# GpSimd's split subtractions moved to VectorE, and three small steps rewritten, in a fused two-layer kernel

## The chip, the cores and the metric

One core of a Trainium2 chip runs the whole program in one launch. The metric is the device time of an execution in microseconds (us). The engines are TensorE (PE, with its weight loads PEld), VectorE (DVE), ScalarE (ACT), GpSimd (POOL) and SyncE (SP, which here only issues transfers).

## The reference, cut to what matters

Everything is float32, with 256 tokens of width 1024. Two layers, each a mixer and a layer of experts, are followed by a block of attention and feed-forward.

```python
for i in range(2):
    h = mlstm_mixer(x, ...) if i == 0 else gla_mixer(x, ...)
    x = layer_norm(ALPHA * x + h, ln_g[i, 0], ln_b[i, 0])
    y = ec_moe(x, ...)            # router, top-32 tokens for each of 16 experts, gate/up/down
    x = layer_norm(ALPHA * x + y, ln_g[i, 1], ln_b[i, 1])
return second_block(x, ...)       # rms norm, attention, rms norm, convolution, gated feed-forward

def mlstm_mixer(x, w_in, gate_b, norm_g, w_out):     # 4 heads, both directions
    z = x @ w_in                                     # q, k, v, o, gates
    logD = where(mask, b[t] - b[s] + i[s], -inf)     # causal mask (mirrored when going backwards)
    s = (q k^T) * exp(logD - m)                      # E = exp(logD - m) is what the kernel calls E
    h = head_norm(s v / max(|den|, exp(-m)))
    return (sigmoid(o) * h) @ w_out

def gla_mixer(x, w_in, gate_w, gate_b, norm_g, w_out):   # gated linear attention, both directions
    loga = log_sigmoid(...) / 16                     # per key channel, so decays are products over time
    ...
    return (silu(r) * head_norm(o)) @ w_out
```

## The kernel before

**Matmuls in three passes.** Each float32 operand of a large projection is split into a high part h (rounded to the matmul's format fp32r) and a low part l = src - h, and `mm3` (L331) issues h*h, h*l and l*h: L332, L333, L334. Activations are xh, xl; weights wh, wl. `split_w` (L287) makes h and l of half a weight unit, 128x1024 elements: ScalarE copies h (L297; in six cases VectorE, L295) and the engine at the end of the list `sub` subtracts (L298). `sub` is set to one of the lists of `ENG`: 0 is VectorE alone, 1 GpSimd alone, 2 both in turn.

**Weights** come as 1 MB units, in one stream, into a pool of 25 slots (`slab()` for activations and `take()` for units draw on the same slots). SP issues the next unit as soon as a slot is free, so a unit's release by its reader starts a transfer.

**Order of the work.** The program is written stage by stage and a scheduler sets the order of each engine's instructions; engines then run their own list in that order.

**The first mixer** (`mlstm`, L510): projections of q and k (transposed, `proj_T`), gates, E for both directions (L574 on VectorE, exp on ScalarE at L576, the triangular masks by GpSimd's affine_select at L580), scores L587 times E (L588 to L591), projection of v, heads (L613 to L621), head norm, then `mixer_out` (L483): projection of the output gate, product, output projection `token_out`. `columns` (L1107), called in between, turns small parameters into columns and multiplies the router's weights by the norm's gain and bias (L1114, GpSimd, tile `rw` in the slab `gpad`); L1124 sums these tables over the 1024 rows with 16 matmuls by a matrix of ones.

**The second mixer** (`gla`, L625) has seven levels in which chunk pairs of doubled length are joined: at each level ScalarE copies k (L706), TensorE multiplies (L715, later L719), and `upd` (L726) multiplies four strided halves of the slabs `kst` and `qs` in place by decay products (L731, four instructions of 128x512 elements per level); L741 makes the next products. The projections of v and of the output gate stand between the levels on TensorE.

**The expert layers** (`moe`) stream 192 units each. At their end `last_down` sums the last expert's output and calls `split_early`, which splits the first one and a half units of what follows, and `norm_split` (L1067) makes the layer norm: statistics, `rsqrt` (L435, nine VectorE instructions on 128x2 values, L442 to L452), a diagonal matrix (L1082), (x - mean) * gain (L1090), a transposing matmul (L1093), and the split into h (ScalarE, L312) and l (VectorE, L313). After it `finish0` and `finish1` make the normalised rows with GpSimd (L1173; L1227 and L1228).

Of the kernel before, what the change touches and what calls it, by code (L numbers as in the profile page):

```python
# [10 lines left out]
F32 = mybir.dt.float32  # L11
# [3 lines left out]
AF = mybir.ActivationFunctionType  # L15
OP = mybir.AluOpType
# [28 lines left out]
def two_layer_mixer_moe_then_attention_kernel(  # L45
# [254 lines left out]

    def transposed(src, use, bank=aux):
# [41 lines left out]

    def split_early():
        open_split()
        sub[:] = ENG[1]
        early.append(iter(list(split_unit())))
        ws = split_unit()
        early.insert(0, chain([next(ws)], ws))
        sub[:] = [nc.vector]  # L350

    def proj_T(xh, xl):
        lo_last = len(early) > 1
        if len(early) == 1 and not tr[1:]:
            tr.append(0)
            wl_last = 1
        else:
            wl_last = 0
        ws = early.pop() if early else split_unit()
        pb = acc()  # L360
        for f in range(2):
            wh, wl = next(ws)
            o = pb[:, f * S:(f + 1) * S]
            if f < lo_last:
                for k in range(8):
                    nc.tensor.matmul(o, wh[:, k, :], xh[:, k, :], start=k == 0, stop=False)
                    mm = nc.tensor.matmul(o, wl[:, k, :], xh[:, k, :], start=False, stop=False)
                for k in range(8):
                    with tc.issue_after(mm.ins):
                        mm = nc.tensor.matmul(o, wh[:, k, :], xl[:, k, :], start=False, stop=k == 7)  # L370
                last[:] = [mm]
                continue
            if wl_last:
# [12 lines left out]
        return pb  # L386
# [96 lines left out]
    def mixer_out(hv, g, func, xh, xl, res, mm, late, ac):  # L483
# [9 lines left out]
        sub[:] = ENG[1]  # L493
# [15 lines left out]
        sub[:] = ENG[2]  # L509
# [5 lines left out]
    def mlstm(xh, xl, res, after_qk):  # L515
# [37 lines left out]

        qk = slab()
# [13 lines left out]
        for d in range(2):  # L568
            e = slab()
# [7 lines left out]
            for h in range(4):  # L577
                for o0 in (0, 256):
                    sg = 1 if d == 0 else -1
                    nc.gpsimd.affine_select(ev[:, h, o0:o0 + P], ev[:, h, o0:o0 + P], pattern=[[sg, P]],  # L580
                                            compare_op=OP.is_ge, fill=0.0, base=0, channel_multiplier=-sg)
            E.append(ev)
# [42 lines left out]
        return mixer_out(hv, V_MLSTM_G, AF.Sigmoid, xh, xl, res, mm, [2, 4], ac)  # L625


    def gla(xh, xl, x1, prep):
# [38 lines left out]
        sub[:] = [(nc.vector, nc.gpsimd)[j] for j in [0, 1]]  # L667
# [26 lines left out]
        for lev in range(7):  # L694
# [31 lines left out]
            def upd(eng, base, d, half, g, ghalf):  # L726
                dst = bass.AP(tensor=base.tensor, offset=base.offset + d * 1024 + half * hh,
                              ap=[list(base.ap[0]), [2 * hh, nb], [1, hh]])
                src = bass.AP(tensor=gprod.tensor, offset=gprod.offset + g * gs + ghalf,
                              ap=[list(ga[0]), [2, nb], [0, hh]])  # L730
                eng.tensor_tensor(dst, dst, src, op=OP.mult)  # L731
# [37 lines left out]
        sub[:] = ENG[2]  # L769
# [19 lines left out]
        return mixer_out(hv, V_GLA_G, AF.Silu, xh, xl, x1, mm, [2, 3], mm)  # L789
# [276 lines left out]
    def norm_split(sums, bn, o, gb, bc, mm):  # L1066
# [13 lines left out]
        for t in range(2):  # L1080
            ts = slice(t * P, (t + 1) * P)
            dgi = nc.vector.tensor_scalar(dg[:, ts], ident, rs2[:, t:t + 1], None, op0=OP.mult)  # L1082
        for t in range(2):
            rs = rs2[:, t:t + 1]
            ts = slice(t * P, (t + 1) * P)
            for c in range(2):
                for u in (2 * c, 2 * c + 1):
                    us = slice(256 * u, 256 * u + 256)
                    with tc.issue_after(dgi.ins):
                        nc.vector.scalar_tensor_tensor(o[:, t, us], sums[u][:, t, :], mv[:, t, 0:1], gb[:, us],  # L1090
                                                       op0=OP.subtract, op1=OP.mult)
                for k in range(4 * c, 4 * c + 4):
                    nc.tensor.matmul(pvs[2 * t + c][:, k % 4, :], o[:, t, k * P:(k + 1) * P], dg[:, ts],  # L1093
                                     start=False, stop=k % 4 == 3)
                hi = split_part(h[:, 4 * c:4 * c + 4, ts], l[:, 4 * c:4 * c + 4, ts], pvs[2 * t + c])
            mvs.append(mv[:, t, :])
            rss.append(rs)
# [9 lines left out]
    def columns():  # L1107
# [4 lines left out]
        for i in range(2):  # L1112
            for j, v in ((1, V_LN_B), (0, V_LN_G)):
                nc.gpsimd.tensor_tensor(rw[:, i, :, j, :], rw[:, i, :, 0, :],  # L1114
                                        cols[:, v + 16 * i:v + 16 * i + 8, None].to_broadcast([P, 8, 16]), op=OP.mult)
            nc.gpsimd.tensor_copy(rt[:, 8 * i:8 * i + 8, :], rw[:, i, :, 0, :])
# [5 lines left out]
        for i in range(2):  # L1122
            for k in range(8):
# [4 lines left out]
        nc.vector.tensor_copy(rsum.rearrange("p i a e -> p (i a e)"), pb[:, :64])  # L1128
# [357 lines left out]
```

## Time and profile before

| | |
|---|---|
| median of 3 runs | 1531.09 us (1530.36 to 1531.26) |
| the profiled execution | 1529.58 us, of which the span of its instructions is 1527.8 us |
| mean granted TensorE clock | 0.869 of full speed |
| busy: PE, PEld | 1304.0 us (85%), 916.9 us (60%) |
| busy: DVE, ACT, POOL | 551.7 us (36%), 374.9 us (25%), 203.7 us (13%) |
| read from HBM | 489.61 MB, 321 GB/s over the span |

How to read the rows further down. A row of the timeline is: start us, duration us, engine, line, operation, what it writes <- what it reads, shape, xcount of instructions merged into it, and in brackets how long the engine was idle before it and who ended that. A row of the windows is: stretch, its length, then busy us and (xcount) of PE, PEld, DVE, ACT, POOL, then the granted TensorE clock, the busy share of the 16 DMA engines, and GB/s. Of the waits: who waited for whom, us in total, times, longest. Of the groups: line, engine, operation, names, shapes, xcount | busy us, mean ns of one | idle before. A float32 matmul that is not fp32r stands as two or more passes in the counts of PE.

### The profile page before, as it was taken

The page shows a single profiled execution, that of the slowest core. Times are in us where ns is not written, and L with a number is a line of the kernel's source. Part 1 is how long each engine was busy: PE and PEld are TensorE (multiplying, and loading weights), DVE is VectorE, ACT ScalarE, POOL GpSimd, SP SyncE. Part 2 cuts the span into 40 slices and gives each one's busy share as a digit, 9 for nine tenths or more (in the row PEclk, how much of TensorE's full clock was granted, in tenths as well). Part 3 has the DMA queues.
Part 4 walks back from the last instruction along what each step waited for, and adds up shares of the span by engine and source line. Part 5 has one row for each costly group of instructions (what it writes and reads, how often), then busy time and mean ns, then how long its engine had stood idle before and what let it go on. Part 6 is the DMA issues. An engine that isn't in the chain of part 4 may idle for free.

```text
span 1527.8 us, 27209 instructions
## 1 busy us (share of the span) xinstructions
PE 1304.0 (85%) x11779; PEld 916.9 (60%) x11779; DVE 551.7 (36%) x1103; ACT 374.9 (25%) x601; POOL 203.7 (13%) x142
## 2 busy tenths in 40 slices
PE   9899977667667677989996758999998899999998
PEld 8787644222222225878753426666564798799997
DVE  5467110011001005686520100200111685687776
ACT  5244100000000001655310000000000365365554
POOL 1243002100100001543100210000002400011000
PEclk9899998677677779999998776867679899999999
DMA  9749899999999999736899999999999943646500
GB/s 287 299 165 359 345 420 421 420 421 421 399 421 421 421 420 356 247 112 249 318 414 421 420 413 421 420 421 420 420 420 387 356 153 106 217 146 203 182 1 28
DMA packets 129303, 492.42 MB, mean 322 GB/s; under 512 B 11570, under 2 KB 68037, under 8 KB 81056
## 3 DMA queue, kind: packets, MB, share of 16 engines
q1 hardware_dynamic: 127216, 489.93, 81.7%
q8 instruction: 92, 1.51, 0.4%
q0 software_dynamic: 864, 0.66, 0.2%
q10 hardware_dynamic: 1104, 0.10, 0.1%
q14 instruction: 27, 0.22, 0.0%
HBM read 489.61 MB, written 1.05 MB: 321 GB/s over the span
## 4 chain that ended last, share of the span: by engine, by line
PE 53%; DMA 36%; DVE 8%; ACT 2%; issue 1%; POOL 0%; SPq 0%; DVEq 0%; ACTq 0%
DMA unit<-in_moe_w_up_dram 13%; DMA unit<-in_moe_w_down_dram 11%; DMA unit<-in_moe_w_gate_dram 11%; PE acc L964 8%; PE acc L333 7%; PE acc L332 7%; PE acc L334 7%; PE aux L1197 6%; PE aux L1011 4%; PE aux L333 1%; PE aux L332 1%; PE aux L334 1%; DVE slab L731 1%; PE aux L919 1%; PE aux L1029 1%
## 5 line engine op out<-in xcount | busy, mean ns | idle before, releaser
L964 PE MATMUL acc<-unit,slab 128*32 128x256 f32 x3840 | 317.5, 472 | 107.5 <-DMA unit<-in_moe_w_up_dram 56.1
L964 PEld LDWEIGHTS acc<-unit,slab 128*32 128x32 f32 x3840 | 129.9, 129 | 291.4 <-DMA unit<-in_moe_w_up_dram 89.8
L333 PE MATMUL acc<-slab 128*128 128x256 f32 (+1 forms) x912 | 282.7, 310 | 3.8 <-DVE slab L298 3.6
L332 PE MATMUL acc<-slab 128*128 128x256 f32 (+1 forms) x912 | 277.9, 310 | 2.1 <-DVE slab L295 1.4
L334 PE MATMUL acc<-slab 128*128 128x256 f32 (+1 forms) x912 | 278.9, 309 | 0.5 <-DVE slab L313 0.3
L297 ACT ACTIVATE slab<-unit 128x1024 fp32r<-128x1024 f32 x158 | 166.0, 1057 | 216.4 <-PE acc L333 69.2
L298 DVE TENSOR_TENSOR slab<-unit,slab 128x1024 fp32r<-128x1024 f32 x125 | 170.8, 1369 | 75.3 <-ACT slab L297 65.9
L1011 PE MATMUL aux<-unit,w 128*32 128x256 f32 x1920 | 154.5, 456 | 47.0 <-DMA unit<-in_moe_w_down_dram 35.8
L333 PEld LDWEIGHTS acc<-slab 128*128 128x128 f32 x912 | 174.7, 192 | 15.2 <-DVE slab L298 4.4
L332 PEld LDWEIGHTS acc<-slab 128*128 128x128 f32 x912 | 174.5, 191 | 11.5 <-ACT slab L677 1.6
L334 PEld LDWEIGHTS acc<-slab 128*128 128x128 f32 x912 | 174.6, 192 | 9.1 <-DVE slab L313 0.7
L980 DVE TENSOR_TENSOR w<-w,acc 128x256 f32<-128x256 f32 x32 | 13.5, 421 | 361.8 <-PE acc L964 348.7
L1011 PEld LDWEIGHTS aux<-unit,w 128*32 128x32 f32 x1920 | 62.6, 125 | 113.3 <-DMA unit<-in_moe_w_down_dram 57.2
L1023 ACT COPY slab<-aux 32x256 f32<-32x256 f32 x60 | 21.7, 361 | 427.3 <-PE aux L1011 426.4
L298 POOL TENSOR_TENSOR slab<-unit,slab 128x1024 fp32r<-128x1024 f32 x37 | 93.5, 2536 | 210.2 <-ACT slab L297 194.0
L1023 DVE COPY slab<-aux 32x256 f32<-32x256 f32 x60 | 25.4, 424 | 230.3 <-ACT slab L1023 229.9
L1197 PEld LDWEIGHTS aux<-slab 33*128 33x128 f32 x512 | 88.3, 267 | 14.7 <-issue 14.7
L1197 PE MATMUL aux<-slab 33*128 33x16 f32 x512 | 90.8, 324 | 0.0
L979 ACT ACTIVATE w<-acc 128x256 f32<-128x256 f32 x32 | 12.3, 383 | 274.1 <-PE acc L964 274.1
L328 POOL DMA_DIRECT2D slab<-in_ln_g_dram x2 | 1.2, 597 | 329.2 <-DMA unit<-in_moe_w_down_dram 243.7
L1388 POOL TENSOR_TENSOR slab<-slab 128x512 fp32r<-128x512 f32 x10 | 18.8, 1883 | 180.5 <-ACT slab L1387 180.5
L919 PEld LDWEIGHTS aux<-slab 128*128 128x128 f32 x192 | 31.6, 210 | 8.9 <-issue 7.8
(344 smaller groups left out, 1332.6 us busy)
## 6 DMA issues: line engine op xcount, KB each, us to landing
unit<-in_moe_w_gate_dram SPq DMA_DIRECT2D x128, 1024.0 KB, 19.8
unit<-in_moe_w_up_dram SPq DMA_DIRECT2D x128, 1024.0 KB, 19.8
unit<-in_moe_w_down_dram SPq DMA_DIRECT2D x128, 1024.0 KB, 19.8
unit<-in_w_up_dram SPq DMA_DIRECT2D x22, 1024.0 KB, 5.3
unit<-in_gla_w_in_dram SPq DMA_DIRECT2D x12, 1024.0 KB, 12.5
unit<-in_w_qkv_dram SPq DMA_DIRECT2D x12, 1024.0 KB, 12.1
unit<-in_mlstm_w_in_dram SPq DMA_DIRECT2D x11, 1024.0 KB, 13.6
unit<-in_w_down_dram SPq DMA_DIRECT2D x11, 1024.0 KB, 4.9
```

The lines of the kernel that those rows point to most:

```text
L297: nc.scalar.activation(h, src, AF.Copy)
L298: eng.tensor_tensor(l, src, h.bitcast(F32), op=OP.subtract)
L332: nc.tensor.matmul(o, ah, bh, start=first, stop=False)
L333: nc.tensor.matmul(o, ah, bl, start=False, stop=False)
L334: last[:] = [nc.tensor.matmul(o, al, bh, start=False, stop=stop)]
L731: eng.tensor_tensor(dst, dst, src, op=OP.mult)
L919: nc.tensor.matmul(o, n_cols(t, k), ohf[:, t], start=t == 0, stop=t == 1)
L964: mm = nc.tensor.matmul(pb[32 * j:32 * j + 32, :256], picked(kk, e), unit[:, k, 256 * j:256 * j + 256], start=kk == 0, stop=kk == 7)
L1011: mm = nc.tensor.matmul(py[32 * j:32 * j + 32, :256], hT[:, kk % 2, 32 * (kk // 2):32 * (kk // 2) + 32], unit[:, k, 256 * j:256 * j + 256] ...
L1023: eng(yb[32 * eg:32 * eg + 32, g % 2, 256 * j:256 * j + 256], py[32 * j:32 * j + 32, :256])
L1197: nc.tensor.matmul(pb[:, 16 * j:16 * j + 16], cb[:, 256 - c:384 - c], relT, start=True, stop=True)
L1388: (nc.vector if p == NP - 1 else nc.gpsimd).tensor_tensor(sl, g, sh.bitcast(F32), op=OP.subtract)
```

## The change

Six edits: (1) all low parts of weights in both mixers, and behind both expert layers, are subtracted by VectorE (37 instructions of GpSimd; none of L298 is left there). (2) Behind an expert layer `split_early` only makes the three high parts; the low parts wait in a list `lows` and `norm_split` issues them behind its own work, one before its four l parts and two after. `norm_split` goes through the columns in the outer loop. `proj_T` orders the first projections by wh*xh, wl*xh, wh*xl. (3) The masks of E become a constant slab `ban` (0 or 1.0e4), made early by GpSimd and taken in VectorE's maximum; the 16 affine_selects of 128x128 go. (4) The router's tables are multiplied by VectorE, copied by ScalarE, and summed by one matmul of 512 columns and a VectorE reduction. (5) `upd` does two halves at once: 14 instructions of 1024 elements per partition in place of 28 of 512. (6) The second copy of k for `gla` is ScalarE's, from PSUM, and not GpSimd's.

```diff
+    def split_hi(src):
...
+        nc.scalar.activation(h, src, AF.Copy)
+        lows.append((l, src, h))
+        return h, l
+
+    def split_low():
+        l, src, h = lows.pop(0)
+        return nc.vector.tensor_tensor(l, src, h.bitcast(F32), op=OP.subtract)
...
     def split_early():
         open_split()
-        sub[:] = ENG[1]
-        early.append(iter(list(split_unit())))
-        ws = split_unit()
-        early.insert(0, chain([next(ws)], ws))
-        sub[:] = [nc.vector]
+        early.append(iter([split_hi(h) for h in halves_of(take())]))
+        a, b = halves_of(take())
+        early.insert(0, chain([split_hi(a)], (split_w(h) for h in (b,))))
...
-    def mixer_out(hv, g, func, xh, xl, res, mm, late, ac):
+    def mixer_out(hv, g, func, xh, xl, res, mm, late, ac, eng=(1, 2)):
...
-        sub[:] = ENG[1]
+        sub[:] = ENG[eng[0]]
...
-        sub[:] = ENG[2]
+        sub[:] = ENG[eng[1]]
...
-                    nc.vector.tensor_scalar(ev[:, h, o0:o0 + n], mbv[:, h, d, t0:t0 + n],
-                                            acol[:, s, d, h:h + 1], 0.0, op0=OP.subtract, op1=OP.max)
+                    b0 = (256 if n == P else P) if d else 0
+                    nc.vector.scalar_tensor_tensor(ev[:, h, o0:o0 + n], mbv[:, h, d, t0:t0 + n],
+                                                   acol[:, s, d, h:h + 1], ban[:, b0:b0 + n],
+                                                   op0=OP.subtract, op1=OP.max)
...
-                    nc.gpsimd.tensor_copy(kv[:, 1, cs], kv[:, 0, cs])
+                    nc.scalar.activation(kv[:, 1, cs], pb, AF.Copy)
...
-            upd(nc.vector, kst, 0, 0, 0, 1)
-            upd(nc.vector, kst, 1, 1, 1, 0)
-            upd(nc.vector, qs, 1, 1, 0, 0)
-            upd(nc.vector, qs, 0, 0, 1, 1)
...
+            upd(kst, 1, gs - 1)
+            upd(qs, gs + 1, -gs - 1)
...
+        dv = then(split_low)
+        for args in todo:
+            dv = then(nc.vector.tensor_sub, *args)
+        while lows:
+            dv = then(split_low)
...
-                nc.gpsimd.tensor_tensor(rw[:, i, :, j, :], rw[:, i, :, 0, :],
+                nc.vector.tensor_tensor(rw[:, i, :, j, :], rw[:, i, :, 0, :],
...
-        for i in range(2):
-            for k in range(8):
-                nc.tensor.matmul(pb[:, 32 * i:32 * i + 32], ones, rw[:, i, k].rearrange("p a e -> p (a e)"),
-                                 start=k == 0, stop=k == 7)
+        nc.tensor.matmul(pb, ones, gpad[:, 1536:2048], start=True, stop=True)
+        nc.vector.tensor_reduce(rsum.rearrange("p i a e -> p i (a e)"),
+                                pb.rearrange("p (i k c) -> p i c k", i=2, k=8), axis=mybir.AxisListType.X, op=OP.add)
```

The order of the changed kernel has its own line numbers: 570 and 572 make `ban`, 585 is the broadcast of L565, 298 the low parts, 313 those of `split_low`, 1102 `then`, 748 `upd`, 756 the next products (L741), 761 L746.

GpSimd between its start and the first expert layer, before; the row ISA without names stands where its kind of instruction changes.

```order
L565 ISA
L565 ISA slab<-slab 128x512 x4
L580 AFFINE_SELECT slab<-slab 128x128 x8
L1114 ISA
L1114 TENSOR_TENSOR slab<-slab,cols 128x8x16 x2
L580 AFFINE_SELECT slab<-slab 128x128 x8
L1114 TENSOR_TENSOR slab<-slab,cols 128x8x16 x2
L1116 COPY rt<-slab 128x128 x2
L298 TENSOR_TENSOR slab<-unit,slab 128x1024 x12
```

The same place in the changed kernel.

```order
L269 MEMSET slab 128x1 x3
L570 MEMSET slab 128x384
L572 AFFINE_SELECT slab<-slab 128x128 x2
L585 ISA
L585 ISA slab<-slab 128x512 x4
L943 DMA slab<-in_ln_g_dram 1x16x64
```

GpSimd keeps the broadcast and goes from there straight to the expert layer's rows; table products, masks and low parts have left it.

VectorE behind the first expert layer, from the diagonal matrices on, before.

```order
L1082 TENSOR_SCALAR w_3909<-ident,rs_y 128x128 x2
L1090 SCALAR_TENSOR_TENSOR slab<-acc,ln_mv_3910,slab 128x256 x2
L1090 SCALAR_TENSOR_TENSOR slab<-aux,ln_mv_3910,slab 128x256 x2
L1090 SCALAR_TENSOR_TENSOR slab<-acc,ln_mv_3910,slab 128x256 x2
L1090 SCALAR_TENSOR_TENSOR slab<-aux,ln_mv_3910,slab 128x256 x2
L313 TENSOR_TENSOR slab<-acc,slab 128x4x128 x2
L313 TENSOR_TENSOR slab<-aux,slab 128x4x128 x2
L638 COPY w_4039<-acc 128x256
```

The same place in the changed kernel.

```order
L1096 TENSOR_SCALAR w_3883<-ident,rs_y 128x128 x2
L1102 SCALAR_TENSOR_TENSOR slab<-acc,ln_mv_3884,slab 128x256 x4
L1102 SCALAR_TENSOR_TENSOR slab<-aux,ln_mv_3884,slab 128x256 x4
L313 TENSOR_TENSOR slab<-unit,slab 128x1024
L1102 TENSOR_TENSOR slab<-acc,slab 128x4x128
L1102 TENSOR_TENSOR slab<-aux,slab 128x4x128
L1102 TENSOR_TENSOR slab<-acc,slab 128x4x128
L1102 TENSOR_TENSOR slab<-aux,slab 128x4x128
L313 TENSOR_TENSOR slab<-unit,slab 128x1024 x2
```

One weight low part has come in front of the four l parts and two behind them.

VectorE at the second and third level of `gla`, before.

```order
L741 TENSOR_TENSOR slab<-slab 128x1024
L731 TENSOR_TENSOR slab<-slab 128x512 x2
L746 COPY_PREDICATED w_4251<-slab,aux 128x256
L741 TENSOR_TENSOR slab<-slab 128x512
L731 TENSOR_TENSOR slab<-slab 128x256x2 x2
L298 TENSOR_TENSOR slab<-unit,slab 128x1024
L731 TENSOR_TENSOR slab<-slab 128x128x4 x2
L731 TENSOR_TENSOR slab<-slab 128x256x2 x2
```

The same levels in the changed kernel.

```order
L756 TENSOR_TENSOR slab<-slab 128x1024
L298 TENSOR_TENSOR slab<-unit,slab 128x1024
L748 TENSOR_TENSOR slab<-slab 128x2x512
L761 COPY_PREDICATED w_4228<-slab,aux 128x256
L756 TENSOR_TENSOR slab<-slab 128x512
L748 TENSOR_TENSOR slab<-slab 128x2x256x2
L298 TENSOR_TENSOR slab<-unit,slab 128x1024 x2
L748 TENSOR_TENSOR slab<-slab 128x2x128x4
L748 TENSOR_TENSOR slab<-slab 128x2x256x2
```

Each pair of L731 has become one L748, and low parts that GpSimd made stand between the levels.

## Rows read from the trace of the kernel before

**Rows 1.** Windows: the first experts' stream and the second mixer's levels.

```profile
194.00:564.00 370.00, 252.48 (x2566) 103.14 (x2565) 35.93 (x80) 17.77 (x46) 24.48 (x23) 0.75 1.01 418
638.00:699.00 61.00, 49.92 (x648) 43.29 (x649) 51.74 (x55) 30.75 (x41) 32.05 (x15) 0.97 0.34 117
```

**Rows 2.** Waits of TensorE in 28:60, 592:652, 652:700 and 1184:1300.

```profile
PE aux L1124 <- POOL slab L1114: 6.6, 1, 6.6
...
PE acc L1093 <- DVE slab L1090: 6.1, 1, 6.1
PE acc L333 <- DVE slab L298: 1.8, 1, 1.8
PE acc L332 <- DVE slab L295: 1.4, 1, 1.4
...
PE aux L715 <- DVE slab L731: 3.8, 2, 3.0
PE aux L764 <- DVE slab L731: 2.4, 1, 2.4
PE acc L333 <- DVE slab L298: 1.7, 1, 1.7
...
PE acc L1093 <- DVE slab L1090: 4.3, 1, 4.3
```

**Rows 3.** Windows at the first expert matmuls of each layer: the DMA share.

```profile
156.00:160.00 4.00, 4.00 (x48) 2.79 (x52) 0.90 (x3) 1.13 (x3) 0.00 (x0) 1.00 0.02 4
...
755.00:760.00 5.00, 5.00 (x60) 3.30 (x60) 0.93 (x3) 1.08 (x3) 0.00 (x0) 1.00 0.19 29
```

**Rows 4.** Windows behind TensorE's longer waits: the granted clock.

```profile
58.40:65.40 7.00, 7.00 (x33) 6.93 (x33) 0.00 (x0) 0.00 (x0) 0.78 (x3) 0.50 1.02 420
...
604.30:610.50 6.20, 6.20 (x33) 6.20 (x34) 4.29 (x10) 1.79 (x3) 0.00 (x0) 0.60 1.05 385
...
680.00:685.00 5.00, 4.61 (x84) 4.58 (x85) 4.84 (x11) 1.82 (x3) 0.00 (x0) 0.66 0.60 211
```

**Rows 5.** Timeline of GpSimd and TensorE around the router's tables, and L1077.

```profile
55.25 0.76 POOL L1114 TENSOR_TENSOR slab<-slab,cols 128x128 f32<-128x128 f32 x2 [7.40 <-issue]
...
58.40 7.04 PE L1124 MATMUL aux<-slab,ones 128*128 128x32 f32 x32 [6.57 <-POOL slab L1114]
...
65.71 4.95 PE L587 MATMUL aux<-slab 128*128 128x256 f32 x12
...
594.61 1.88 PE L1077 MATMUL acc<-cols,ident 128*128 128x512 f32 x4
```

**Rows 6.** Timeline of GpSimd and VectorE in the norm behind the first experts.

```profile
595.19 6.95 POOL L298 TENSOR_TENSOR slab<-unit,slab 128x1024 fp32r<-128x1024 f32 x3 [90.46 <-ACT slab L297]
...
595.90 1.66 DVE L442 TENSOR_SCALAR rs_w<-ln_mv 128x2 f32<-128x2 f32 x1
...
602.19 0.16 DVE L449 TENSOR_TENSOR rs_q<-rs_q,rs_w 128x2 f32<-128x2 f32 x1
```

**Rows 7.** VectorE: groups in 28:60, 76:118 and 636:700, and one row of its timeline.

```profile
L574 DVE TENSOR_SCALAR slab<-slab,acol 128x256 f32<-128x256 f32 x8 | 2.8, 349 | 1.3 <-POOL slab L565 1.3
...
L618 DVE TENSOR_TENSOR den<-den,ecol 128x2 f32<-128x2 f32 x8 | 7.7, 960 | 0.1
L621 DVE SCALAR_TENSOR_TENSOR slab<-aux,den,slab 128x256 f32<-128x256 f32 x8 | 3.9, 484 | 3.9 <-ACT slab L620 3.8
...
L731 DVE TENSOR_TENSOR slab<-slab 128x512 f32<-128x512 f32 x28 | 26.1, 976 | 4.1 <-PE aux L719 3.5
L298 DVE TENSOR_TENSOR slab<-unit,slab 128x1024 fp32r<-128x1024 f32 x4 | 7.4, 1866 | 0.0
...
658.29 1.21 DVE L298 TENSOR_TENSOR slab<-unit,slab 128x1024 fp32r<-128x1024 f32 x1
```

**Rows 8.** Timeline behind the second experts: GpSimd's rows and VectorE's low parts.

```profile
1215.00 6.73 POOL L1228 TENSOR_TENSOR slab<-slab 128x1024 f32<-128x1024 f32 x2
...
1213.42 9.39 DVE L298 TENSOR_TENSOR slab<-unit,slab 128x1024 fp32r<-128x1024 f32 x3 [4.32 <-DMA unit<-in_w_qkv_dram]
```

More of the change, by code (lines that the diff above doesn't have):

```diff
@@ L299, in split_w @@
         return h, l
+    lows = []
+    def split_hi(src):
+        t = wsp.pop()
+        wsp.insert(0, t)
+        h, l = (t[:, 1024 * i:1024 * i + 1024].rearrange("p (k f) -> p k f", k=src.shape[1]) for i in range(2))
+        nc.scalar.activation(h, src, AF.Copy)
[4 more added lines that the diff above has]
+        return nc.vector.tensor_tensor(l, src, h.bitcast(F32), op=OP.subtract)
     def transposed(src, use, bank=aux):
@@ L342, in split_unit, with halves_of @@
         return (split_w(unit[:, :, f * P:(f + 1) * P]) for f in range(2))
+    def halves_of(unit):
+        return [unit[:, :, f * P:(f + 1) * P] for f in range(2)]
     def split_early():
         open_split()
-        sub[:] = ENG[1]
-        early.append(iter(list(split_unit())))
-        ws = split_unit()
-        early.insert(0, chain([next(ws)], ws))
-        sub[:] = [nc.vector]
+        early.append(iter([split_hi(h) for h in halves_of(take())]))
+        a, b = halves_of(take())
+        early.insert(0, chain([split_hi(a)], (split_w(h) for h in (b,))))
     def proj_T(xh, xl):
@@ L364, in proj_T @@
             if f < lo_last:
-                for k in range(8):
[L366 to L370, printed above, removed]
+                mm = None
+                for i, (w, x) in enumerate(((wh, xh), (wl, xh), (wh, xl))):
+                    for k in range(8):
+                        with tc.issue_after(mm.ins) if mm is not None else ExitStack():
+                            mm = nc.tensor.matmul(o, w[:, k, :], x[:, k, :], start=i + k == 0, stop=i == 2 and k == 7)
                 last[:] = [mm]
                 continue
-            if wl_last:
+            if wl_last or lo_last:
                 for k in range(8):
@@ L552, in gates @@
             return mr, acol, ecol, mbv
+        es = [slab()]
+        ban = es[0][:, 1536:1920]
+        nc.gpsimd.memset(ban, 0.0)
+        for o0, sg in ((0, 1), (256, -1)):
+            nc.gpsimd.affine_select(ban[:, o0:o0 + P], ban[:, o0:o0 + P], pattern=[[sg, P]], compare_op=OP.is_ge,
+                                    fill=1.0e4, base=0, channel_multiplier=-sg)
         qk = slab()
@@ L568, in mlstm @@
         for d in range(2):
-            e = slab()
+            e = es[0] if d == 0 else slab()
             ev = e[:, :1536].rearrange("p (h b) -> p h b", h=4)
@@ L666, in gla @@
         his[:] = [0, 0, 1, 1, 1, 1][::-1]
-        sub[:] = [(nc.vector, nc.gpsimd)[j] for j in [0, 1]]
+        sub[:] = ENG[0]
         for j in range(5):
@@ L724, in gla, with upd @@
             gs = ga[1][0]
[L726 to L731, printed above, removed]
-            upd(nc.vector, kst, 0, 0, 0, 1)
-            upd(nc.vector, kst, 1, 1, 1, 0)
-            upd(nc.vector, qs, 1, 1, 0, 0)
-            upd(nc.vector, qs, 0, 0, 1, 1)
+            def upd(base, off, step):
+                dst = bass.AP(tensor=base.tensor, offset=base.offset,
+                              ap=[list(base.ap[0]), [1024 + hh, 2], [2 * hh, nb], [1, hh]])
+                src = bass.AP(tensor=gprod.tensor, offset=gprod.offset + off,
+                              ap=[list(ga[0]), [step, 2], [2, nb], [0, hh]])
+                nc.vector.tensor_tensor(dst, dst, src, op=OP.mult)
+            upd(kst, 1, gs - 1)
+            upd(qs, gs + 1, -gs - 1)
             if lev < 6:
@@ L1081, in norm_split, with then @@
             ts = slice(t * P, (t + 1) * P)
[L1082 to L1086, printed above, removed]
+            dv = nc.vector.tensor_scalar(dg[:, ts], ident, rs2[:, t:t + 1], None, op0=OP.mult)
+            mvs.append(mv[:, t, :])
+            rss.append(rs2[:, t:t + 1])
+        def then(step, *args, **kw):
+            with tc.issue_after(dv.ins):
+                return step(*args, **kw)
+        todo = []
+        for c in range(2):
+            ks = slice(4 * c, 4 * c + 4)
+            for t in range(2):
+                ts = slice(t * P, (t + 1) * P)
                 for u in (2 * c, 2 * c + 1):
                     us = slice(256 * u, 256 * u + 256)
-                    with tc.issue_after(dgi.ins):
-                        nc.vector.scalar_tensor_tensor(o[:, t, us], sums[u][:, t, :], mv[:, t, 0:1], gb[:, us],
-                                                       op0=OP.subtract, op1=OP.mult)
+                    dv = then(nc.vector.scalar_tensor_tensor, o[:, t, us], sums[u][:, t, :], mv[:, t, 0:1], gb[:, us],
+                              op0=OP.subtract, op1=OP.mult)
+                pv = pvs[2 * t + c]
                 for k in range(4 * c, 4 * c + 4):
-                    nc.tensor.matmul(pvs[2 * t + c][:, k % 4, :], o[:, t, k * P:(k + 1) * P], dg[:, ts],
+                    nc.tensor.matmul(pv[:, k % 4, :], o[:, t, k * P:(k + 1) * P], dg[:, ts],
                                      start=False, stop=k % 4 == 3)
-                hi = split_part(h[:, 4 * c:4 * c + 4, ts], l[:, 4 * c:4 * c + 4, ts], pvs[2 * t + c])
-            mvs.append(mv[:, t, :])
-            rss.append(rs)
+                hi = nc.scalar.activation(h[:, ks, ts], pv, AF.Copy)
+                todo.append((l[:, ks, ts], pv, h[:, ks, ts].bitcast(F32)))
+        dv = then(split_low)
[3 more added lines that the diff above has]
+            dv = then(split_low)
         return h, l, mvs, rss, hi
```

15 lines of the change are left out of this document (4 added, 11 removed).

## The prediction

> **What bounds the kernel now.** I read first the windows by stage. In the first experts' stream the DMA engines are busy for all of the time (share 1.01 at 418 GB/s) and TensorE for 252.48 of 370 us; in the levels of the second mixer the DMA share is 0.34, and TensorE (49.92 of 61 us) and VectorE (51.74) are both nearly full [rows 1]. So the expert layers are bound by their transfers, the mixers by chains of engines, and the change touches only mixers and the steps behind expert layers. Does a faster mixer help, if a stream of transfers follows? The reader should look at the stretch in which the first expert matmuls run: there the DMA engines stand at a share of 0.02 and 0.19 with TensorE at 1.00 of its clock [rows 3]. All slots are full and the stream waits for TensorE to release them, so its start moves with the mixer, and what a mixer saves comes out at the end. Next the waits of TensorE: 6.6 us for the router's tables made by GpSimd, 6.1 and 4.3 for the norms behind the two expert layers, and five between 1.4 and 3.8 us in the second mixer, 11.1 together [rows 2]. [...]
>
> The last view is the timeline of VectorE. Its L442 on two elements per partition takes 1.66 us while GpSimd makes low parts (595.19 to 602.14), and L449 on the same size 0.16 us right after them, at 602.19 [rows 6]. Likewise L618 at 960 ns for 128x2, L731 at 976 for 128x512 and L298 at 1866 in the levels, but 1.21 us alone [rows 7]. An instruction of VectorE that reads only SBUF is held for as long as a GpSimd instruction of 2.3 us (6.95 for three [rows 6]) runs.
>
> **The change part by part.**
>
> A, first mixer. Gone are the wait of 6.6 us [rows 2], which stands behind 7.40 us in which GpSimd waits for nothing the profile shows [rows 5]; most of L1124's 7.04 us [rows 5], for which one matmul of 512 columns remains (L1077 takes 1.88 us for four rows, so 0.5 to 1.9, taken as 1.0); and half of L587's 4.95 us, which follow at the low clock [rows 4, 5], taken as 2.0 of 2.5. That is 6.6 + 6.0 + 2.0 = 14.6. Against it VectorE gets the eight low parts of the output gate's projection, 8 x 1.21 = 9.7, and loses the hold on L618, 7.7 - 8 x 0.16 = 6.4 [rows 6, 7]. Of the 3.3 left I take 0.6 as late for TensorE, which has the heads' matmuls and the high passes to do meanwhile. A is 14.0, with ends 10 (3.3 in full and the wait half replaced by one for VectorE's tables) and 15. The new mask operand costs VectorE at most what L621, also with two tensors, takes over L574, (484 - 349) ns x 16 = 2.2 us [rows 7]; it is hidden by TensorE's projections, and if not, is inside the lower end. The four table products, ScalarE's copies of `rt` and the reduction behind the matmul have the same cover. The constant `ban` is made at the start, when GpSimd has nothing else. GpSimd's one DMA of norm gains behind the broadcast is wanted only by the experts.
>
> [...]
>
> B, norm behind the first experts. From L442's start at 595.90 to L449's at 602.19 are 6.3 us, in which three instructions start that would take 0.2 each: 5.7 gone of the wait of 6.1 [rows 2, 6]. The 6.20 us of L1093 that follow ran at 0.60 [rows 4], and would take 3.7 at 1.00: 2.5 more, if the shorter wait leaves the clock up. One low part of 1.21 now stands ahead of the four l parts, which TensorE needs behind its first passes only: 0.5 to 0.7 late. B is 7.5, ends 5.7 and 8.3. Late next is then the norm's own chain on VectorE.
>
> C, second mixer. At most the 11.1 us of waits go [rows 2], and of the 4.61 us at clock 0.66 a third, 1.6 [rows 4]: 12.7, which leaves TensorE 48.3 us busy. What VectorE has in the 61 us afterwards: 51.74, less 28 L731 at 976 ns (26.1), plus 14 merged at some 1.2 (16.8, the price of L298 alone, which also reads two tensors of 1024), less 7.4 for its four low parts, plus 15 low parts at 1.21 (18.2, eleven of them GpSimd's so far) [rows 1, 7]: 53.2, and less for what the other 18.2 us lose in holds, down to 43. With VectorE at 50 the stage is 50 long and the gain 11; with 53.2 and none of its gaps closed it is 4, with VectorE below TensorE 12.7. I take 11, since all rows of these 18.2 stand beside GpSimd's. The second copy of k costs ScalarE the same copy once more; it is busy for 30.75 of 61 us [rows 1]. Late next are low parts, for TensorE's L333.
>
> D, norm behind the second experts. Of the 4.3 us wait [rows 2] the hold is as large a part as of the first, 5.7 of 6.1, so 4.0, and the clock gives 2.4 as in B: 6.4. But here GpSimd still has L1227 and L1228, four instructions, of which two took 6.73 us, and three low parts beside them took VectorE 9.39, that is 3.1 each [rows 8]. The moved low parts fall on them: two of these holds, 2 x (3.1 - 1.2) = 3.8, and 0.1 for the order, come back in front of the projections. D is 2.5, ends 0 and 6.4.
>
> [...]
>
> Sum: 14.0 + 7.5 + 11.0 + 2.5 = 35.0. From the profiled execution's 1529.58 that is 1494.6; the median of the runs, 1531.09, stands 1.5 above it, so 1496. All upper ends give 42.4 at most, all lower 19.7.
>
> **The rivals.** (1) VectorE becomes the bound of the mixers, as all that leaves GpSimd comes to it. For it: 51.74 of 61 us now, and 53.2 by the prices without relief [rows 1]. Against it: the holds seen in every group [rows 6, 7]. Then C is 3, A 11, D 0 and B stays 7.5: 21.5 won, 1509. (2) The transfers swallow part. Once a mixer ends so early that the units before the experts have not all landed, nothing more is won. The idle stretches are about 4 us and 4 us long [rows 3]; with D that caps the gain at some 10.5, 1520. Against it: the DMA share of 0.34 in the levels [rows 1], in which the fill could be done earlier, since slots are released earlier too. (3) Slower: VectorE's long instructions are not GpSimd's doing but its own, and low parts stay at 1.87 and merged products at twice 976. Then C loses 26.1 + 15 x 1.87 + 18.2 - 61 = 11; A gains nothing (8 x 1.87 = 15); the first four low parts of an output projection cost 7.5, and the one in front of each norm's l parts 1.9: 22 slower in all, 1553. It decides from the point where the low parts put more on VectorE's path than the 24 us of A, B and D. Against it is the 1.21 us of the same instruction alone [rows 7]. (4) The gains in A are taken back by a later wait and the rest hides: within 0.2%, about 3 us, which is what a measurement of this kernel can tell from no change. That the change does not do what it says is excluded by the order: no low part is left on GpSimd.
>
> **How the numbers follow.** Forecast 0.66, with a range of its own of 1488 to 1504 (42.4 with the top ends; 27 where two terms lie low). VectorE bound 0.20, transfers 0.08, slower 0.04, no change 0.02. The likeliest is 1496. The range reaches up to 1512 to take in rival 1 with its 1509, and ends at 1486, leaving out (2), (3), (4) and a little on both sides. Faster: 0.66 + 0.20 + 0.08 = 0.94, same 0.02, slower 0.04.
>
> **What would show it.** A: no wait before the table matmul, and a clock near 1.00 in L587 behind it. B: all instructions of the reciprocal root at 0.16 us, TensorE's wait at L1093 under 1 us, and L1093 near 3.7. C: merged products at about 1.2, low parts at 1.21, the stage near 50 long; if VectorE is the bound, TensorE waits there for low parts or merged products and VectorE is over 95% busy. D: low parts of some 3 us beside L1227. The transfers: the DMA share at the first expert matmuls; no idle stretch left there means rival 2. I would be wrong if TensorE waited for low parts in the output projections, or if merged products took 2 us.

## The result and the profile after

The changed kernel takes 1492.55 us (1491.23 to 1493.73) against 1530.72 of the kernel before, measured beside it: a ratio of 0.9752, 95% interval 0.9735 to 0.9769, or 38.2 us less where 35 were forecast. Its profiled execution is one of 1491.23 us with a span of 1489.5, against 1527.8. Times here are of executions at the usual clock: one of the run that gives three low parts back to GpSimd took 1963.29 us at a mean granted clock of 0.547 and is left out of its median.

Where the 38.3 us of span went is read from the start, or where it says so the end, of the same matmuls in both timelines. Each stretch runs from the mark in the line above to its own.

| mark (TensorE) | before | after | stretch shorter by | forecast |
|---|---|---|---|---|
| first matmul of the first experts | 156.87 | 142.68 | 14.2 | A 14.0 |
| first bias matmul of the norm (L1077, now L1091) | 594.61 | 583.18 | -2.8 | 0 |
| end of the norm's matmuls (L1093, now L1115) | 610.50 | 592.25 | 6.8 | B 7.5 |
| first product with v (L784, now L798) | 698.62 | 667.39 | 13.0 | C 11.0 |
| first matmul of the second experts | 755.78 | 724.60 | 0.0 | 0 |
| first bias matmul of the second norm | 1193.50 | 1159.64 | 2.7 | 0 |
| end of that norm's matmuls | 1207.75 | 1167.49 | 6.4 | D, the gain: 6.4 |
| end of the span | 1527.8 | 1489.5 | -2.0 | D, given back: -3.9 |

Waits of TensorE in the whole changed kernel, cut to those that answer to [rows 2] and the new ones.

```profile
PE aux L1058 <- issue: 3.9, 3, 3.1
...
PE acc L346 <- ACT slab L326: 2.8, 3, 2.1
...
PE aux L779 <- DVE slab L748: 2.3, 1, 2.3
PE aux L1276 <- DVE rs_y L457: 1.4, 1, 1.4
...
PE acc L384 <- DVE slab L1102: 0.9, 1, 0.9
...
PE acc L1115 <- DVE slab L1102: 0.8, 2, 0.4
```

The 6.6 us for the tables is gone, the 10.4 for the two norms is 0.8, and of the second mixer's 11.1 the 2.3 at L779 are left. Waits for nothing that the profile shows ("issue") are 3.9 us at L1058, where the kernel before has 1.8 at L1057 and 0.2 at L1044, both ahead of a norm. New are two waits behind the second experts (L1276, L384) and, in the first mixer, 2.1 us for ScalarE's L326 at the head of the output projection.

Windows of the changed kernel: behind the table matmul, in the norm, in the levels, and at the first expert matmuls of both layers.

```profile
54.00:61.00 7.00, 7.00 (x31) 5.35 (x30) 5.29 (x15) 1.06 (x1) 0.00 (x0) 1.00 1.03 420
587.20:592.20 5.00, 5.00 (x45) 4.43 (x45) 5.00 (x11) 1.79 (x3) 0.00 (x0) 1.00 1.05 384
...
624.80:667.40 42.60, 40.27 (x566) 35.72 (x551) 37.51 (x44) 24.97 (x34) 0.00 (x0) 1.00 0.44 150
142.00:146.00 4.00, 4.00 (x51) 2.71 (x54) 0.93 (x3) 0.97 (x3) 0.00 (x0) 1.00 0.09 14
722.00:726.00 4.00, 4.00 (x37) 3.32 (x39) 0.65 (x3) 0.88 (x3) 0.00 (x0) 1.00 0.08 29
```

The clock is 1.00 where [rows 4] had 0.50, 0.60 and 0.66. In the levels TensorE is busy for 40.27 of 42.60 us and VectorE for 37.51, so TensorE bounds them. The DMA engines still stand nearly idle ahead of each expert stream, at a share of 0.09 (142 to 146 us) and 0.08 (722 to 726): the transfers swallowed nothing.

The table matmul takes 1.02 us, with no wait before it:

```profile
53.79 1.02 PE L1148 MATMUL aux<-slab,ones 128*128 128x512 f32 x2
```

Timeline of VectorE in the norm behind the first experts, after.

```profile
584.47 0.17 DVE L456 TENSOR_SCALAR rs_w<-ln_mv 128x2 f32<-128x2 f32 x1
...
589.78 1.21 DVE L313 TENSOR_TENSOR slab<-unit,slab 128x1024 fp32r<-128x1024 f32 x1
```

The reciprocal root starts at 0.17 us an instruction, where [rows 6] had 1.66 for the first. Groups of VectorE in the levels (624 to 668), after:

```profile
L748 DVE TENSOR_TENSOR slab<-slab 128x1024 f32<-128x1024 f32 x14 | 17.0, 1219 | 0.5 <-PE aux L732 0.2
L298 DVE TENSOR_TENSOR slab<-unit,slab 128x1024 fp32r<-128x1024 f32 x13 | 15.8, 1218 | 3.8 <-ACT slab L297 3.7
```

Merged updates and low parts cost 1.22 us each, as priced; [rows 7] had 976 ns for half the size and 1866.

The 13.0 us of the second mixer do not all lie in its levels. From the norm's end to the first matmul of the levels (L715, now L732) it is 39.90 us before and 32.51 after, and from there to the first product with v 48.22 and 42.63: 7.4 us are won ahead of the levels and 5.6 in them.

### The profile page after: what moved, and what is told of

It reads as the page before. It is cut to its first block, busy times and chain, and to the rows that moved or that the text cites. A ratio compares the mean times of both kernels' runs of the same rounds, so it can differ in the third digit from the quotient of the medians.

```text
span 1489.5 us, 27080 instructions
## 1 busy us (share of the span) xinstructions
PE 1288.0 (86%) x11749; PEld 906.5 (61%) x11749; DVE 552.3 (37%) x1130; ACT 376.3 (25%) x605; POOL 105.0 (7%) x84
## 4 chain that ended last, share of the span: by engine, by line
PE 52%; DMA 42%; DVE 4%; POOL 1%; issue 1%; ACT 1%; DVEq 0%; SPq 0%; ACTq 0%; POOLq 0%
DMA unit<-in_moe_w_down_dram 16%; DMA unit<-in_moe_w_up_dram 13%; DMA unit<-in_moe_w_gate_dram 12%; PE acc L347 8%; PE acc L346 8%; PE acc L348 8%; PE acc L978 6%; PE aux L1222 4%; PE aux L1025 3%; PE aux L346 1%; PE aux L347 1%; PE aux L348 1%; PE aux L933 1%; PE aux L630 1%; PE aux L1043 1%
## 5 line engine op out<-in xcount | busy, mean ns | idle before, releaser
L347 PE MATMUL acc<-slab 128*128 128x256 f32 (+1 forms) x896 | 276.7, 309 | 0.6 <-DVE slab L298 0.4
L346 PE MATMUL acc<-slab 128*128 128x256 f32 (+1 forms) x896 | 273.4, 310 | 2.8 <-ACT slab L326 2.8
L348 PE MATMUL acc<-slab 128*128 128x256 f32 (+1 forms) x896 | 273.9, 309 | 0.0
L298 DVE TENSOR_TENSOR slab<-unit,slab 128x1024 fp32r<-128x1024 f32 x156 | 198.7, 1279 | 81.0 <-ACT slab L297 79.1
L297 ACT ACTIVATE slab<-unit 128x1024 fp32r<-128x1024 f32 x152 | 160.2, 1058 | 154.1 <-PE acc L347 75.7
L346 PEld LDWEIGHTS acc<-slab 128*128 128x128 f32 x896 | 170.8, 191 | 12.8 <-ACT slab L326 3.6
L347 PEld LDWEIGHTS acc<-slab 128*128 128x128 f32 x896 | 170.9, 191 | 11.0 <-issue 1.7
L348 PEld LDWEIGHTS acc<-slab 128*128 128x128 f32 x896 | 170.9, 191 | 8.7 <-issue 1.1
L1222 PEld LDWEIGHTS aux<-slab 33*128 33x128 f32 x512 | 91.7, 276 | 14.2 <-issue 14.2
L1222 PE MATMUL aux<-slab 33*128 33x16 f32 x512 | 94.0, 331 | 0.0
L933 PE MATMUL aux<-slab 128*128 128x128 f32 (+1 forms) x192 | 35.7, 329 | 0.0
L347 PE MATMUL aux<-slab 128*128 128x512 f32 x88 | 34.3, 390 | 0.0
L348 PE MATMUL aux<-slab 128*128 128x512 f32 x88 | 34.2, 389 | 0.0
```

The lines of the kernel that those rows point to most:

```text
L297: nc.scalar.activation(h, src, AF.Copy)
L298: eng.tensor_tensor(l, src, h.bitcast(F32), op=OP.subtract)
L346: nc.tensor.matmul(o, ah, bh, start=first, stop=False)
L347: nc.tensor.matmul(o, ah, bl, start=False, stop=False)
L348: last[:] = [nc.tensor.matmul(o, al, bh, start=False, stop=stop)]
L933: nc.tensor.matmul(o, n_cols(t, k), ohf[:, t], start=t == 0, stop=t == 1)
```

## The experiments

Each was timed beside the kernel before; differences under 3 us are read from the marks in the timelines. No run separates edit 6, or the order of the first projections in edit 2, from the rest.

**One part alone, on the kernel before.** The engine lists, everywhere (the first line in `split_early` and for the output gate, the second for the output projections and v, the third for the gates' part of `gla`):

```diff
-        sub[:] = ENG[1]
+        sub[:] = ENG[0]
...
-        sub[:] = ENG[2]
+        sub[:] = ENG[0]
...
-        sub[:] = [(nc.vector, nc.gpsimd)[j] for j in [0, 1]]
+        sub[:] = ENG[0]
```

> The kernel before with one part of the change: every low part of weights goes to VectorE, by the engine lists alone; tables, masks, level updates and the norm's order stay as before. Theory 1 (each edit has its gain in its own stage, and the stages add): the table step keeps its wait of some 6.6 us, the three low parts stand in front of the norms' statistics (3.6 us instead of holds of 5.7 and 4.0 us), the levels win 8 to 11: about 17 us less than before, 1514. Theory 2 (nearly all of the gain is GpSimd's hold on VectorE, the other edits are incidental): at least 30 us less, 1500 or under. Theory 3 (low parts only change the queue they stand in): within 4 us of before.

Measured: 1514.1 us, ratio 0.9897 (0.9884 to 0.9910), as theory 1 had it. But the parts fell otherwise. The table wait stayed at 6.6 us and the first expert matmul at 157.58. From the first norm's bias matmul on, the norm won 2.1 us, the second mixer up to v 10.6, the second norm 6.1; and the second expert layer lost 5.1. That loss, in the timeline of VectorE and then of TensorE at its end:

```profile
1180.58 1.23 DVE L298 TENSOR_TENSOR slab<-unit,slab 128x1024 fp32r<-128x1024 f32 x1 [5.02 <-ACT slab L297]
```
```profile
1184.72 2.08 PE L1056 MATMUL aux<-slab 128*128 128x256 f32 x4 [5.46 <-DVE slab L1050]
```

An early low part on VectorE waits 5.02 us for its high part, and with it the copies of the last expert's result (L1050) behind it, for which TensorE waits 5.46. So moving the low parts alone is not enough: the list `lows`, which holds them back until the norm's own work is done, takes this wait away.

The tables alone (edit 4 in the kernel before, as in the diff above):

> The kernel before with one part of the change: the router's tables are multiplied by VectorE, copied by ScalarE and summed by one matmul and a reduction; masks and low parts stay with GpSimd. Theory 1: the whole of the first mixer's gain, 12 to 14 us, is this step: 1517 to 1519, and the first expert matmul comes 12 to 14 us earlier than at 156.9. Theory 2: 5 us at most, since VectorE's own products would be held beside GpSimd's masks and low parts.

Measured: 1514.58 us, ratio 0.9898 (0.9885 to 0.9910): 15.2 us less, and the first expert matmul at 142.94, 13.9 earlier. Theory 2 falls: this one step (products and copies off GpSimd, and the sum in one matmul) brings the first mixer's whole gain, with masks and low parts still on GpSimd. Together the two parts bring 15.7 + 15.2 = 30.9 of the 38.2 us.

**One part undone, in the changed kernel.** GpSimd makes the three early low parts again:

```diff
-        early.append(iter([split_hi(h) for h in halves_of(take())]))
+        sub[:] = ENG[1]
+        early.append(iter(list(split_unit())))
...
-        dv = then(split_low)
         for args in todo:
```

> The changed kernel, with the three low parts behind each expert layer made by GpSimd again, at once with the high parts, as before; the rest of the norm keeps its new order. Theory 1: the holds on the reciprocal root return (5.7 and 4.0 us) and with them the low clock (2.5 and 2.4), less 1.9 us for the low parts that no longer stand on VectorE: 12 to 13 us over the changed kernel, 1505. Theory 4 (the new order inside the norm is what helps, not the engine): under 5 us over it, 1497 or less.

Measured: 1505.1 us, ratio 0.9833 (0.9820 to 0.9845), 12.6 over the changed kernel. Theory 4 falls, the sum is that of theory 1, and the hold is back. GpSimd, then VectorE:

```profile
581.25 6.96 POOL L298 TENSOR_TENSOR slab<-unit,slab 128x1024 fp32r<-128x1024 f32 x3 [89.56 <-DMA unit<-in_gla_w_in_dram]
```
```profile
584.86 1.08 DVE L458 TENSOR_SCALAR rs_w<-ln_mv 128x2 f32<-128x2 f32 x1
585.98 2.27 DVE L459 TENSOR_SCALAR rs_y<-rs_w 128x2 int32<-128x2 int32 x1
```

L459 ends at 588.25, GpSimd's three at 588.21. TensorE waits 3.4 us there, and 3.3 in the second norm. By the marks the two norms are 4.5 and 4.3 us longer, 8.8 where theory 1 had 12 to 13. The stretch of the second experts is 3.9 us longer too, with a pause of 1.83 in it of the kind discussed below; theory 1 does not explain that, and the agreement of the sum is in part luck.

GpSimd takes every other low part of the second mixer's gates and of v, and then also those of its output gate and output projection (the last pair of lines, in the second run only):

```diff
-        sub[:] = ENG[0]
+        sub[:] = [(nc.vector, nc.gpsimd)[j] for j in [0, 1]]
...
+        sub[:] = ENG[2]
...
-        return mixer_out(hv, V_GLA_G, AF.Silu, xh, xl, x1, mm, [2, 3], mm, (0, 0))
+        return mixer_out(hv, V_GLA_G, AF.Silu, xh, xl, x1, mm, [2, 3], mm, (1, 2))
```

> The changed kernel, with the low parts of the second mixer's projections up to v alternating between VectorE and GpSimd again, as before; the level updates stay merged. Theory 1 (GpSimd's holds make the levels long): 8 to 11 us over the changed kernel, 1501 to 1504, merged updates near 1.9 us each. Theory 5 (merging the updates is what shortens the levels): 0 to 3 us over it, merged updates near 1.2.

> The changed kernel with all low parts of the second mixer divided as before, those of the output gate and output projection too, which stand between the levels; updates stay merged. Theory 1 (low parts on GpSimd between the levels hold VectorE there): the levels are 4 to 6 us longer again, on top of the 5 us of the gates' part alone: 9 to 12 us over the changed kernel, 1501 to 1505. Theory 5 (the merged updates make the levels short): 5 us over it, 1497, as with the gates' part alone.

Measured: 1497.54 us (ratio 0.9786, 0.9773 to 0.9798) and 1500.77 (0.9807, 0.9793 to 0.9820; 9.6 over the changed kernel measured beside it). The first missed both theories: its 5 us lie ahead of the levels (38.0 in place of 32.5 us from the norm's end to the first level), since only seven low parts went to GpSimd and two of them fall into the levels. With the other parts the levels themselves grow from 42.6 us to 46.6, although the updates stay merged. From the norm's end to v this run takes 84.6 us, against 75.1 in the changed kernel and 88.1 before: the low parts' engine accounts for 9.4 of the 13.0 us. The groups of VectorE in the levels of the second run:

```profile
L748 DVE TENSOR_TENSOR slab<-slab 128x1024 f32<-128x1024 f32 x14 | 25.0, 1796 | 2.9 <-PE aux L736 1.8 <-PE aux L732 0.4
```

Updates unmerged (28 of 512 elements per partition), and in another run also the masks by affine_select as before:

> The changed kernel, with the level updates unmerged again (28 of 512 elements per partition in place of 14 of 1024), all low parts on VectorE. Theory 1: 28 at some 0.68 us are 19 us against 17.0, so VectorE gets 2 us more beside a nearly full TensorE: 0 to 2 us over the changed kernel, 1493 to 1495. Theory 5 (merging is what shortens the levels): 8 to 11 us over it.

> The changed kernel, with the triangular masks again made by GpSimd's affine_select behind the exponential. Theory 1: the masks are not on the path, TensorE has projections to do: within 2 us of the changed kernel. Theory 10 (the 16 masks stand between exponential and scores, and hold VectorE): 4 us or more over it, with a wait of TensorE or VectorE for GpSimd near the scores.

> The changed kernel with two of its edits undone together: masks by GpSimd's affine_select again, and 28 unmerged level updates. Theory 12 (neither edit gives anything; the 3.8 us by which the unmerged form was faster are the pause of 3.1 us that its program does not have): levels as long as in the changed kernel, 1486 to 1491 with or without the pause. Theory 5 or 10 (one of them is worth something that the other hid): over 1495.

Measured: 1488.73 us (ratio 0.9739, 0.9726 to 0.9752), 1490.64 (0.9743, 0.9729 to 0.9756) and 1488.76 (0.9730, 0.9717 to 0.9743). Merging brings nothing: from the norm's end to v the unmerged kernel takes 75.16 us and the merged 75.14. Its updates in the levels:

```profile
L748 DVE TENSOR_TENSOR slab<-slab 128x512 f32<-128x512 f32 x28 | 18.1, 690 | 0.7 <-PE aux L736 0.3
```

Nor do the masks: with them on GpSimd the first expert matmul comes at 142.01. So theories 5 and 10 fall. The unmerged kernels are lower by 2 to 4 us, about the limit of 0.2%; their stretch of the first experts is 2.9 and 2.5 us shorter, since they lack a pause (below).

Table products by GpSimd, with masks and low parts gone from it:

```diff
-                nc.vector.tensor_tensor(rw[:, i, :, j, :], rw[:, i, :, 0, :],
+                nc.gpsimd.tensor_tensor(rw[:, i, :, j, :], rw[:, i, :, 0, :],
...
-            nc.scalar.copy(rt[:, 8 * i:8 * i + 8, :], rw[:, i, :, 0, :])
+            nc.gpsimd.tensor_copy(rt[:, 8 * i:8 * i + 8, :], rw[:, i, :, 0, :])
```

> The changed kernel, with the four table products and the copies of the table made by GpSimd again; the sum stays one matmul. GpSimd has no masks and no low parts in the first mixer any more. Theory 6 (GpSimd's stop of 7.4 us with the change of the kind of its instructions makes the tables late): TensorE waits 3 to 7 us before the table matmul, and the low clock behind it adds 2: 4 to 9 us over the changed kernel. Theory 7 (the tables were late because masks stood ahead of them in GpSimd's queue): no wait, within 2 us of the changed kernel.

Measured: 1492.34 us (ratio 0.9759, 0.9746 to 0.9772), equal to the changed kernel, with no wait for the table. Theory 7, but with the other's mechanism in it; GpSimd's timeline:

```profile
35.91 4.87 POOL L585 PARTITION_BROADCAST slab<-slab  x4 [32.89 <-DVE slab L553]
47.79 3.32 POOL L1140 TENSOR_TENSOR slab<-slab,cols 128x128 f32<-128x128 f32 x4 [7.02 <-issue]
```

The stop of 7 us between the broadcast and the first product is still there. It now begins at 40.8, and not behind masks (before, 7.40 us up to 55.25 [rows 5]), and the products are ready at 51.1 us, before TensorE comes to them at 52.7. That it was masks, and not low parts, that stood ahead follows from the run with the engine lists alone, where the low parts have left GpSimd and the wait stays at 6.6 us. The stop has no releaser in either kernel (7.40 and 7.02 us), and no run here shows what GpSimd does in it.

The sum by 16 matmuls again:

> The changed kernel, with the tables again summed by 16 matmuls of 32 columns; the products stay on VectorE. Theory 8 (most of those matmuls' 7.04 us was the low clock after the wait): at full clock they take 3.5 us, 2.5 over the one matmul and its 1.0: 2 to 3 us over the changed kernel. Theory 9 (16 short matmuls that change their weights take their 7 us at any clock): 6 us over it.

```profile
53.14 3.66 PE L1150 MATMUL aux<-slab,ones 128*128 128x32 f32 x32
```

Measured: 1495.03 us (ratio 0.9773, 0.9760 to 0.9787). With no wait before them the 16 take 3.66 us, and in the kernel before 7.04 at a clock of 0.50 [rows 4, 5]: by that, 3.4 us were the clock, as theory 8 had it. The 2.5 us of the medians are a coincidence, though: the first expert matmul is 5.1 us later, and 3 us come back since this run lacks the pause. Of the 5.1, 2.6 are lost at the sum and most of the rest at the scores behind it (L604), whose first 12 take 4.54 us:

```profile
57.00:61.30 4.30, 4.30 (x15) 3.48 (x14) 2.69 (x13) 0.00 (x0) 0.00 (x0) 0.60 1.00 412
```

The clock there is 0.60 although TensorE waited for nothing before it; what it had done was the 16 short matmuls. So the low clock at L587 before [rows 4, 5] is not shown to be the wait's doing: it comes back with those matmuls alone, and the single matmul is part of the gain.

**What is given back behind the second experts.** The four GpSimd instructions that follow its norm are left out:

```diff
-            nc.gpsimd.tensor_tensor(r[:, t, :], r[:, t, :], gb[:, :1024], op=OP.mult)
-            nc.gpsimd.tensor_tensor(r[:, t, :], r[:, t, :], gb[:, 1024:2048], op=OP.add)
```

> The changed kernel without the four GpSimd instructions behind the second experts that multiply the normalised rows by the gain and add the bias; the residual of the last block lacks them. Theory 13 (the low parts beside them are late for nobody): VectorE's three low parts fall from 9.4 us to 3.6 and the time stays within 1 us of the changed kernel's. Theory 14 (the step of the prediction: two holds of 1.9 us come back in front of the projections): 2 to 4 us less.

Measured: 1488.57 us (ratio 0.9734, 0.9721 to 0.9748), 2.6 under the changed kernel measured beside it: the time of theory 14, but not by its mechanism. In the changed kernel GpSimd, VectorE and TensorE read:

```profile
1170.02 7.86 POOL L1252 TENSOR_TENSOR slab<-slab 128x1024 f32<-128x1024 f32 x2 [21.54 <-DVE slab L1102]
1177.84 6.73 POOL L1253 TENSOR_TENSOR slab<-slab 128x1024 f32<-128x1024 f32 x2
```
```profile
1169.92 2.35 DVE L313 TENSOR_TENSOR slab<-unit,slab 128x1024 fp32r<-128x1024 f32 x2
1172.88 9.42 DVE L298 TENSOR_TENSOR slab<-unit,slab 128x1024 fp32r<-128x1024 f32 x3 [0.62 <-ACT slab L297]
...
1182.82 1.78 DVE L460 SCALAR_TENSOR_TENSOR rs_q<-rs_y,rs_w 128x1 f32<-128x1 f32 x1
```
```profile
1168.35 2.62 PE L384 MATMUL acc<-slab 128*128 128x256 f32 x20 [0.87 <-DVE slab L1102]
...
1186.86 0.49 PE L1276 MATMUL aux<-w,ones 128*128 128x128 f32 x2 [1.37 <-DVE rs_y L457]
```

The moved low parts (L313, 1.2 us each) start 0.1 us ahead of GpSimd's first instruction and are not held. GpSimd is: its first two take 7.86 us beside them and the low parts that follow, and took 4.77 in the kernel before:

```profile
1210.27 4.77 POOL L1227 TENSOR_TENSOR slab<-slab 128x1024 f32<-128x1024 f32 x2 [11.19 <-ACT slab L1225]
```

The next three low parts, of the attention's projection, are held (9.42 us for the three), and behind them the reciprocal root of the rms norm, for which L1276 waits 1.37. Without GpSimd's four that wait is gone, and the 0.87 at L384, for an l part behind the first low part, stays. By the marks the end is 2.9 us shorter; 1.4 of that is this wait, and the rest stays open.

**The pause.** The changed kernel once more:

> The changed kernel once more, unaltered, beside the next three. If the pause of 3.1 us in TensorE's list within the last down projection of the first experts belongs to this program, it is there again and the time is 1491 to 1494; if it is chance, it is gone or elsewhere and the profiled execution is some 3 us shorter.

Measured: 1491.2 us (ratio 0.9747, 0.9734 to 0.9761). The pause is there, in the same group of matmuls. First the changed kernel, then the same again:

```profile
570.02 0.97 PE L1058 MATMUL aux<-unit,w 128*32 128x64 f32 x52 [0.76 <-DMA unit<-in_moe_w_down_dram]
574.10 0.42 PE L1058 MATMUL aux<-unit,w 128*32 128x64 f32 x12 [3.10 <-issue]
```
```profile
573.35 0.64 PE L1058 MATMUL aux<-unit,w 128*32 128x64 f32 x12 [2.80 <-issue]
```

It cuts a group of 64 behind the 52nd, and the stretch of the first experts is 2.8 us longer than before. It is there in seven of the ten programs made from the changed kernel (itself among them), and not in the kernel before nor in the two made from that one. The first unmerged kernel lacks it, though its list of TensorE is the same up to this place; so the list alone does not decide it. The kernel before has a pause of its own, at the end of the second experts, and runs the 5.2 us from there to the norm at a clock of 0.67:

```profile
1188.38 0.70 PE L1057 MATMUL acc<-slab 128*128 128x256 f32 x2 [1.77 <-issue]
```

The traces say more of what TensorE waits for. The changed kernel's page of the profile lists transfers of instructions:

```profile
q8 instruction: 92, 1.51, 0.4%
```

That is 92 packets of 16 KB for 23625 records of TensorE (weight loads, matmuls, semaphores), one for every 257. Counted in these records, the long pause comes after the 8385th in all eight executions that have it (with the masks on GpSimd that is behind the 50th of the group, not the 52nd), and the pauses at the end of the second experts, that of the kernel before among them, after the 19137th: 42 x 256 further on. In each of the eight one of the packets starts inside the pause (at 571.52 us in the changed kernel, where TensorE stands from 570.99 to 574.10). In the six executions without it the corresponding packet starts 150 to 240 records sooner, with TensorE at work. So the pause looks like instructions that come late; no run forces it, and why the packet is late in some programs stays open.

## Why the prediction was right

**A** (14.0, measured 14.2). The parts stand: no wait, 1.02 us for the table matmul (L1148), clock 1.00 behind it. GpSimd's stop, on which the 6.6 us rest, is late only because masks stood ahead of it; with the sum in one matmul, taking either the table products or the masks from GpSimd would have sufficed, and the low parts, which the sum weighs against the hold on L618, bring nothing here by themselves (157.58 with the lists alone). The 2.0 us for L587's clock were won, but not as the price of a wait alone: the clock falls behind the 16 short matmuls without one (0.60). The mask operand costs VectorE 480 ns in place of 349 at 128x256 and 347 in place of 281 at 128x128, eight of each, 1.6 us in sum, hidden (the prediction took the larger shape for all 16). For the 128 elements more the new form takes 133 ns and the old one 68, so what an element adds doubles; the rest of each instruction, some 214 ns by these four times, is the same in both forms.

**B** (7.5, measured 6.8). The hold went in full, 5.7 of 6.1 us, and L1115 runs at 1.00. What is missing is the order: twelve matmuls of the next projection, some 1.2 us, now stand between the norm's. Without them B is 8.0.

**C** (11.0, measured 13.0). The direction and the cause were right, GpSimd's holds on VectorE. Of the 13.0, 1.2 are the twelve matmuls that count in B's stretch now, so C itself is 11.8, between the forecast and its upper end of 12.7. VectorE's other work shrank so far (37.51 of 42.60 us in the levels) that TensorE became the bound, which answers rival 1 too. The low parts' engine is shown to bring 9.4 us; the merging, which the sum priced beside it, is worth nothing by itself; some 2.4 are left, which no run divides among the other edits.

**D** (net 2.5, measured 4.4). The gain was 6.4 as worked out. The mis-sized term is "two of these holds, 2 x (3.1 - 1.2) = 3.8": 2.0 us came back, and not by those low parts, which started first, but by waits of 1.37 for the rms norm's root behind the next three and 0.87 for an l part. Each of those three took 3.1 us, 1.9 longer than alone and less than one GpSimd instruction (4.77 for two). The two low parts of which the first started before GpSimd's instruction were not held (2.35 us for both), and none of the three waited longer than one of GpSimd's.

**Not foreseen**: that low parts put early on VectorE would block the expert layer's end (5.1 us in the run with lists alone), which the change avoids; and the pauses in TensorE's list, which cost 2.8 us in the first experts and gave 2.7 in the second, where the pause of 1.77 us and the low clock behind it are gone. That the two cancel, so that the sum came out as if they were not there, is luck.

## What to carry to other kernels

An engine that is busy for 13% of the time can still be what delays another: look for short instructions that last as long as a neighbour's long one, and price a wait together with the clock granted behind it (0.60 over the 6.2 us behind the first norm's wait of 6.1 us, before). When work is moved to an in-order engine, ask what it will itself wait for and what is queued behind it, and hold it back until that work is out. Undo each part of a change by itself: here two edits (the merged updates, the masks in the changed kernel) carry nothing by themselves, and the tables' wait had two sufficient cures.

## What the runs showed of the hardware that was not expected

Between a partition broadcast and the first tensor product after it GpSimd stands for 7.0 to 7.4 us, with eight affine_selects in between (7.40, before) or none (7.02); between a broadcast and an affine_select no such stop was seen (3.56 us, ended by ScalarE), nor where affine_selects and products alternate after the first (no idle time from 55.25 to 58.66 us, before). TensorE paused for 2.8 to 3.15 us in the midst of 64 short matmuls, with no releaser, in the same place in both profiled executions of the changed kernel, with a 16 KB packet of instructions in flight. The prediction says that an instruction of VectorE that reads only SBUF is held by GpSimd's; that is too wide, for the aggregation of the norm's statistics (L1078, from SBUF) takes 0.38 us for two at 595.48, beside the low parts that hold L442, L443 and L448 (1.66, 2.27 and 2.26 us), and the same 0.38 without them (584.06 in the changed kernel). Merging two VectorE instructions of 512 elements into one of 1024 saves 0.16 us (2 x 0.69 against 1.22).
